# Down phase of a transformer block: one of seven products stays in PSUM, weight sums in place, weight buffers opened earlier

## The chip, the core and the metric

The kernel runs on one core of one Trainium2 chip. The metric is the device time of one execution in microseconds (us), as the median of several. PE is TensorE, DVE VectorE, ACT ScalarE, POOL GpSimd and SP SyncE; SP and POOL issue the large transfers.

## The reference

One layer of an encoder, 512 tokens, width 2048, float32:

```
p = rmsnorm(x) @ W_in                  # six groups of 1024 columns
A = differential attention, 8 heads    # softmax(q1 k1) - lam softmax(q2 k2), then rmsnorm per head
N = neighbourhood attention, 8 heads   # banded softmax with a bias
x = x + concat(A, N) @ W_out           # 2048 x 2048
u = rmsnorm(x) @ W_up                  # 2048 x 8192
x = x + square(relu(u)) @ W_down       # 8192 x 2048
out = rmsnorm(x) * g
```

The change touches the last two matrix products and, through the size of shared tiles, the code ahead of them.

## The kernel before

Every float32 operand is split in two fp32r parts: `hi` is a cast on ACT (L94), `lo` is source minus `hi` on DVE (L95). A product then takes three matmuls: hi·hi, hi·lo, lo·hi. For W_up and W_down the kernel computes a 2x2 block product by Strassen's scheme in Winograd's form, with seven products in place of eight, and sums of weight blocks and of operand blocks as the operands.

The stages, in time: projections and attention; the out-projection (to about 841 us); the **up phase** (841 to 1491.5, 32 column groups `q`, each 7 products of 24 matmuls 128x256, L588); the **down phase** (1491.5 to 2156, L741); the end. The down phase runs over 8 chunks `c` of the hidden width and in each over 2 halves `n` of the output columns. A *half* is seven products of 24 matmuls 128x512; the products are named here by their operand, o[0] to o[6]. Each product needs two weight units of 512 KB, each cut into `wh` and `wl`; 12 matmuls go with a unit. There are three buffers each for `wh` and `wl`.

A scheduler orders the instructions of each engine in advance; within that order an engine waits for semaphores. `tc.high_priority` moves weight loads and splits ahead in it. What a tile pool's free space allows decides how far: the pools of the up phase are closed and those of the down phase opened between the two (L617 to L621), and `wd`, with 11 units of 4 KB per partition, holds all weight loads of the down phase.

In a half, products add into three PSUM tiles of two banks, `pU`, `pV`, `pW`. The scheme needs partial sums: `pU` takes o[0], o[2], o[4], o[6] one after the other, and after each the tile is added into its part of `y` (L753, DVE; `y` is the 512x2048 sum in SBUF). Two of the seven results per half leave by another way: a copy to `st` on ACT (L750) and a DMA of POOL that adds it into `y` (L751). The weight sums are made so: t1 is b11 loaded a second time with b12 added by a POOL DMA (L662 to L663), t2 = t1+b22 and t4 = t2+b21 are DVE sums into fresh tiles (L669).

The order of products in a half:

```
prod(pU, o[0], w11, True)   # then copy and DMA into y
prod(pW, o[1], w1, True)
prod(pU, o[2], w2, False)
prod(pW, o[3], next(ops), False)
prod(pU, o[4], next(ops), False)
prod(pV, o[5], next(ops), True)
prod(pU, o[6], next(ops), False)
```

Operands of attention, out-projection, up and down phase share the pool `tpool`: 4 slots of 16 KB per partition. `mixT` (attention's output, the out-projection's operand) has four such tiles, each of two pairs of heads; `mix_pair` (L432 to L438) loads an earlier pair back from DRAM and splits it. At the start of the up phase, L553 to L565 make its seven operands from `H`.

Of the kernel before, what the change touches and what calls it, by code (L numbers as in the profile page):

```python
# [35 lines left out]
def hymba_kernel(ctx: ExitStack, tc: tile.TileContext, x, x_t, norm_mix_g, w_dq, w_dk, w_dv, w_nq, w_nk, w_nv, lams,  # L36
# [5 lines left out]
    tpool = ctx.enter_context(tc.tile_pool(name="tpool", bufs=4))  # L42
# [72 lines left out]
    hT = [tpool.tile([P, 2, 4, SEQ], F32R, name=f"hT{i}", tag="T") for i in range(4)]  # L115

    def hT_k(kt, hl):
        return hT[kt // 4][:, hl, kt % 4, :]
# [32 lines left out]
    with tc.tile_pool(name="start", bufs=4) as sp, tc.high_priority(offset=20000):  # L151
        acc = sp.tile([P, 2 * SEQ], F32, name="acc", bufs=1)
        xs = []
        for u in range(4):
# [8 lines left out]
            for k in range(4):  # L163
                g, hi = gT[:, 4 * u + k:4 * u + k + 1], hT[u][:, 0, k, :]
                nc.scalar.mul(hi, xt[:, k, :], g)
                nc.vector.scalar_tensor_tensor(out=hT[u][:, 1, k, :], in0=xt[:, k, :], scalar=g, in1=hi.bitcast(F32),  # L166
                                               op0=ALU.mult, op1=ALU.subtract)
# [28 lines left out]
    with es:  # L196
# [128 lines left out]
        def mixed(h, i, o):  # L325
# [102 lines left out]
    hpool = up_es.enter_context(tc.tile_pool(name="hpool", bufs=2))  # L428
    early = up_es.enter_context(tc.tile_pool(name="early", bufs=1))

    def mix_pair(h):
        with tc.high_priority(offset=3000):  # L432
            mf = wpool.tile([P, 2, SEQ], F32, name="mf", tag="raw")
            nc.sync.dma_start(out=mf, in_=mixd[h].rearrange("i p s -> p i s"))
            m, ks = mixT[h // 2], slice(h % 2 * 2, h % 2 * 2 + 2)
            nc.scalar.copy(out=m[:, 0, ks, :], in_=mf)
            eng = nc.gpsimd if h % 2 else nc.vector
            eng.tensor_sub(out=m[:, 1, ks, :], in0=mf, in1=m[:, 0, ks, :].bitcast(F32))  # L438


    H = [hpool.tile([P, 2, 8, 256], F32, name=f"H{i}", tag="H") for i in range(2)]

    def operand(pool, name, tag):

        return pool.tile([P, 2, 8, 256], F32R, name=name, tag=tag)

    def split_s(o, src, neg=False, cuts=1):
        n = 8 // cuts
        for i in range(cuts):
            ks = slice(i * n, i * n + n)  # L450
            if neg:
                nc.scalar.mul(o[:, 0, ks], src[:, ks], -1.0)
                nc.vector.scalar_tensor_tensor(out=o[:, 1, ks], in0=src[:, ks], scalar=-1.0,
                                               in1=o[:, 0, ks].bitcast(F32), op0=ALU.mult, op1=ALU.subtract)
            else:
                split(o[:, 0, ks], o[:, 1, ks], src[:, ks])
# [40 lines left out]
    with tc.tile_pool(name="trans", bufs=2) as tr:  # L497
        for n in range(4):
# [7 lines left out]
            for u in range(8):  # L506
# [3 lines left out]
                for t in range(NT):  # L510
                    ts = slice(t * P, (t + 1) * P)
                    for k in range(2):
                        kt = 2 * u + k
                        m = mixT[kt // 4]
# [371 lines left out]
```

## Time and profile before

| | us |
|---|---|
| median of 3 runs | 2173.17 (2172.59 to 2174.12) |
| profiled execution, its own time | 2174.77 |
| its span, first to last instruction | 2173.0 |
| PE busy | 2094.5 (96%) |
| DVE busy | 1544.0 (71%) |
| ACT busy | 988.1 (45%) |
| mean granted clock of TensorE | 0.984 |

The rows and sums below are those of the profiled execution. Its time is 1.77 us more than its span (start and end of the program) and 1.6 us more than the median. A busy PE is read with care: matmul rows overlap, so that what PE lost in a stretch is the stretch less its matmuls times their spacing.

### The profile page before, as it was taken

How to read it: one execution, taken by the hardware profiler on the slowest of the kernel's cores; microseconds unless marked ns; L12 is line 12 of the kernel's file. 1: busy time of each engine (PE TensorE's matmuls, PEld its weight loads, DVE VectorE, ACT ScalarE, POOL GpSimd, SP SyncE). 2: the span in 40 equal slices, each digit the busy share in tenths (PEclk: the TensorE clock that was granted, in tenths of full speed). 3: DMA queues.
4: the chain of work that ended last, by engine and by line, in shares of the span. 5: the costliest groups of instructions: out<-in, count | busy, mean ns of one | idle time of the engine just before them, and what ended most of it. 6: DMA issues, size and time to landing. Idle time of an engine off the chain costs nothing.

```text
span 2173.0 us, 31223 instructions
## 1 busy us (share of the span) xinstructions
PE 2094.5 (96%) x12604; PEld 1867.4 (86%) x12604; DVE 1544.0 (71%) x1710; ACT 988.1 (45%) x1339; POOL 285.1 (13%) x273
## 2 busy tenths in 40 slices
PE   7999999999999998999999999996999999999995
PEld 6989989989888887999999999995787887787874
DVE  6656556556485437778777877775688798789778
ACT  4444444445354534444444444443455455455444
POOL 4221222122221000000000000000111111111110
PEclk8999999999999999999999999998999999999998
DMA  6332232232233731344334434337798999899983
GB/s 213 121 100 90 96 108 86 94 111 78 92 117 116 271 126 59 120 142 141 123 125 146 136 127 136 131 124 235 199 251 232 232 254 246 234 245 240 246 209 111
DMA packets 114417, 340.30 MB, mean 157 GB/s; under 512 B 11808, under 2 KB 28384, under 8 KB 114272
## 3 DMA queue, kind: packets, MB, share of 16 engines
q1 hardware_dynamic: 87360, 257.07, 35.3%
q0 software_dynamic: 26480, 80.70, 17.1%
q8 instruction: 99, 1.62, 0.3%
q10 hardware_dynamic: 432, 0.53, 0.1%
q14 instruction: 46, 0.38, 0.1%
HBM read 291.06 MB, written 30.25 MB: 148 GB/s over the span
## 4 chain that ended last, share of the span: by engine, by line
PE 84%; DMA 6%; DVE 6%; ACT 2%; issue 1%; SPq 0%; ACTq 0%; DVEq 0%; POOLq 0%
PE pm L588 29%; PE pd L741 19%; PE pa L141 8%; PE pa L99 7%; PE pa L98 7%; PE pa L100 7%; DMA b<-in_w_down 6%; DVE wl L95 2%; PE pb L100 1%; PE pb L98 1%; PE pb L99 1%; PE pc L99 1%; PE pc L100 1%; PE pc L98 1%; DVE y L753 1%
## 5 line engine op out<-in xcount | busy, mean ns | idle before, releaser
L741 PE MATMUL pd<-wh,uT 128*128 128x512 f32 x1792 | 558.2, 393 | 9.3 <-ACT wh L94 8.6
L94 ACT CAST wh<-b 128x1024 fp32r<-128x1024 f32 x256 | 268.6, 1049 | 386.2 <-PE pd L741 215.0
L741 PEld LDWEIGHTS pd<-wh,uT 128*128 128x128 f32 x1792 | 339.8, 190 | 81.3 <-ACT wh L94 9.2
L741 PE MATMUL pd<-wl,uT 128*128 128x512 f32 x896 | 354.2, 395 | 31.0 <-DVE wl L95 30.8
L95 DVE TENSOR_TENSOR wl<-b,wh 128x1024 fp32r<-128x1024 f32 x256 | 311.2, 1219 | 62.9 <-ACT wh L94 60.8
L94 ACT CAST wh<-ts 128x1024 fp32r<-128x1024 f32 x192 | 200.0, 1051 | 291.7 <-PE pm L588 180.7
L95 DVE TENSOR_TENSOR wl<-ts,wh 128x1024 fp32r<-128x1024 f32 x192 | 232.7, 1221 | 131.0 <-ACT wh L94 130.7
L588 PE MATMUL pm<-s,wh 128*128 128x256 f32 x1536 | 281.0, 284 | 3.5 <-ACT p L593 2.2
L588 PE MATMUL pm<-a,wh 128*128 128x256 f32 x1536 | 273.9, 282 | 0.8 <-ACT wh L94 0.8
L588 PEld LDWEIGHTS pm<-s,wh 128*128 128x128 f32 x1536 | 239.5, 191 | 3.9 <-ACT p L593 2.4
L588 PEld LDWEIGHTS pm<-a,wh 128*128 128x128 f32 x1536 | 235.0, 189 | 1.0 <-ACT wh L94 1.0
L741 PEld LDWEIGHTS pd<-wl,uT 128*128 128x128 f32 x896 | 169.8, 190 | 75.4 <-DVE wl L95 40.6
L89 ACT CAST wh<-raw 128x1024 fp32r<-128x1024 f32 (+1 forms) x129 | 134.5, 1043 | 200.2 <-PE pa L99 72.1
L588 PE MATMUL pm<-s,wl 128*128 128x256 f32 x768 | 218.3, 284 | 0.0
L141 PE MATMUL pa<-wh,hT 128*128 128x256 f32 x1024 | 201.1, 291 | 14.7 <-DVE hT L166 8.0
L588 PE MATMUL pm<-a,wl 128*128 128x256 f32 x768 | 211.5, 281 | 0.0
L90 DVE TENSOR_TENSOR wl<-raw,wh 128x1024 fp32r<-128x1024 f32 (+1 forms) x98 | 120.9, 1235 | 117.0 <-ACT wh L89 115.6
L100 PE MATMUL pa<-hT,wl 128*128 128x512 f32 x512 | 201.5, 393 | 0.0
L99 PE MATMUL pa<-hT,wh 128*128 128x512 f32 x512 | 201.2, 393 | 0.0
L98 PE MATMUL pa<-hT,wh 128*128 128x512 f32 x512 | 200.7, 392 | 0.0
L141 PEld LDWEIGHTS pa<-wh,hT 128*128 128x128 f32 x1024 | 167.9, 196 | 19.4 <-DVE hT L166 9.4
L141 PE MATMUL pa<-wl,hT 128*128 128x256 f32 x512 | 147.6, 289 | 0.0
(245 smaller groups left out, 3398.9 us busy)
## 6 DMA issues: line engine op xcount, KB each, us to landing
b<-in_w_down SPq DMA_DIRECT2D x160, 512.0 KB, 5.3
b<-in_w_up SPq DMA_DIRECT2D x128, 512.0 KB, 3.6
b<-in_w_down POOLq DMA_DIRECT2D x64, 512.0 KB, 8.4
raw<-in_w_out SPq DMA_DIRECT2D x32, 512.0 KB, 3.5
ud<-c POOLq DMA_DIRECT2D x32, 512.0 KB, 3.2
ur<-ud SPq DMA_DIRECT2D x32, 512.0 KB, 5.3
y<-st POOLq DMA_DIRECT2D x28, 512.0 KB, 8.1
raw<-in_w_dq SPq DMA_DIRECT2D x16, 512.0 KB, 3.3
```

The costliest lines, as they stand in the source:

```text
L89: nc.scalar.copy(out=wh[:, cs], in_=raw[:, cs])
L90: eng.tensor_sub(out=wl[:, cs], in0=raw[:, cs], in1=wh[:, cs].bitcast(F32))
L94: nc.scalar.copy(out=hi, in_=src)
L95: (eng or nc.vector).tensor_sub(out=lo, in0=src, in1=hi.bitcast(F32))
L98: nc.tensor.matmul(out=ps, lhsT=lh, rhs=rh, start=first, stop=False)
L99: nc.tensor.matmul(out=ps, lhsT=lh, rhs=rl, start=False, stop=False)
L100: nc.tensor.matmul(out=ps, lhsT=ll, rhs=rh, start=False, stop=last)
L141: nc.tensor.matmul(out=ps[t], lhsT=a, rhs=b[:, k, :], start=first and i == 0, stop=last and i == 2, skip_group_check=True)
L588: nc.tensor.matmul(out=ps, lhsT=a[:, k], rhs=b[:, k], start=first and k + i == 0, stop=last and k == 7 and i == 2, skip_group_check=True)
L741: nc.tensor.matmul(out=ps[:, b], lhsT=l, rhs=r[:, k], start=first and u + k + i == 0, stop=last and u == 1 and k == 1 and i == 2, skip_gro ...
L753: nc.vector.tensor_tensor(out=ys, in0=ys, in1=ps, op=ALU.subtract if neg else ALU.add)
```

## The change

The operand pool gets 8 slots of 8 KB in place of 4 of 16 KB; `mixT`, `hT` and the up phase's operands become twice as many tiles. `H[1]` gets a pool of its own, which is closed once the up phase's operands are made; in its place a pool `wd` for weights of the down phase is opened, ahead of the up phase's products. In the down phase, the second product of a half (o[1], with the weights b21) adds up in PSUM over all 8 chunks, in a tile `pv` for each `n`, and is added into `y` once, in the last chunk. `pU` and `pW` are two tiles that swap names from half to half, and the other six products go to them in the order pU, pW, pU, pW, pU, pU. The weight sums are made in place: `ch` holds b11, then by a POOL DMA b11+b12, then by DVE adds + b22 and + b21. b11 is thus loaded once instead of twice. The last half finishes `y` in another order.

```
-    tpool = ctx.enter_context(tc.tile_pool(name="tpool", bufs=4))
+    tpool = ctx.enter_context(tc.tile_pool(name="tpool", bufs=8))
     keep = ctx.enter_context(tc.tile_pool(name="keep", bufs=1))
...
-                    mixT.extend(tpool.tile([P, 2, 4, SEQ], F32R, name=f"mixT{m}", tag="T") for m in range(4))
-                split(mixT[kt // 4][:, 0, kt % 4, :], mixT[kt // 4][:, 1, kt % 4, :], o)
+                    mixT.extend(tpool.tile([P, 2, 2, SEQ], F32R, name=f"mixT{m}", tag="T") for m in range(8))
+                split(mixT[h][:, 0, i, :], mixT[h][:, 1, i, :], o)
...
-    hpool = up_es.enter_context(tc.tile_pool(name="hpool", bufs=2))
-    early = up_es.enter_context(tc.tile_pool(name="early", bufs=1))
+    hpool = up_es.enter_context(tc.tile_pool(name="hpool", bufs=1))
+    early = up_es.enter_context(tc.tile_pool(name="early", bufs=2))
...
-    psD = ctx.enter_context(tc.tile_pool(name="psD", bufs=4, space=bass.MemoryType.PSUM, reuse_waits="tile"))
+    psD = ctx.enter_context(tc.tile_pool(name="psD", bufs=2, space=bass.MemoryType.PSUM, reuse_waits="tile"))
     ypool = ctx.enter_context(tc.tile_pool(name="ypool", bufs=1, reuse_waits="tile"))
-    wd = ctx.enter_context(tc.tile_pool(name="wd", bufs=11, reuse_waits="tile"))
+    wd2 = ctx.enter_context(tc.tile_pool(name="wd2", bufs=3, reuse_waits="tile"))
     y = ypool.tile([P, NT, DM], F32, name="y")
...
-        with tc.high_priority(offset=700):
-            u11, u22, u21, u12 = load(0, 0), load(1, 1), load(0, 1), load(1, 0)
-            pairs = [tpool.tile([P, 2, 2, 4, 256], F32R, name="uT", tag="T") for _ in range(4)]
-            o = [pairs[i // 2][:, i % 2] for i in range(7)]
...
+        with tc.high_priority(offset=700 if c else 250):
+            u11, u12, u21, u22 = load(0, 0), load(1, 0), load(0, 1), load(1, 1)
+            o = [part(u11), part(u12)]
+            nc.vector.tensor_sub(out=u21, in0=u22, in1=u21)
+            o.append(part(u21))
+            f = rx.tile([P, 4, 256], F32, name="uf", tag="b")
+            nc.vector.tensor_add(out=f, in0=u11, in1=u22)
+            o.append(part(f, neg=True))
+            nc.vector.tensor_sub(out=f, in0=f, in1=u12)
+            o += [part(f), part(u11), part(u22)]
...
         def add(a, b):
-            with tc.high_priority(offset=ah):
-                t = wpool.tile([P, 1024], F32, name="ts", tag="raw")
-                nc.vector.tensor_add(out=t, in0=a, in1=b)
-            return t
-
...
-        yield [parts(load(u, 0)) for u in range(2)]
-        t1 = [load(u, 0, 1) for u in range(2)]
-        yield [parts(t) for t in t1]
-        b22 = [load(u, 3) for u in range(2)]
-        t2 = [add(t1[u], b22[u]) for u in range(2)]
-        yield [parts(t) for t in t2]
-        yield [parts(t) for t in b22]
-        t3 = [load(u, 3, 1) for u in range(2)]
-        yield [parts(t) for t in t3]
-        b21 = [load(u, 2) for u in range(2)]
-        t4 = [add(t2[u], b21[u]) for u in range(2)]
-        yield [parts(t) for t in b21]
-        yield [parts(t) for t in t4]
...
+            with tc.high_priority(offset=3000):
+                nc.vector.tensor_add(out=a, in0=a, in1=b)
...
+        ch = [load(wd, "ch", u, 0) for u in range(2)]
+        yield parts(ch)
+        for u in range(2):
+            plus(ch[u], u, 1)
+        b21 = [load(wpool, "raw", u, 2) for u in range(2)]
+        yield parts(b21)
+        yield parts(ch)
+        b22 = [load(wd, "b22", u, 3, bufs=3) for u in range(2)]
+        for u in range(2):
+            add(ch[u], b22[u])
+        yield parts(ch)
+        yield parts(b22)
+        t3 = [load(wd2, "t3", u, 3, 1) for u in range(2)]
+        yield parts(t3)
+        for u in range(2):
+            add(ch[u], b21[u])
+        yield parts(ch)
...
-                    finish(t, 0, None, 0)
-                    times_g(t, 0, 1024)
-            w11, w1, w2 = next(ops), next(ops), next(ops)
-            prod(pU, o[0], w11, True)
-            to_y(pU, 0, 0, False, fresh=True, dma=not end)
-            prod(pW, o[1], w1, True)
+                    finish(t, 0, 1024, 0)
+            prod(pU, o[0], next(ops), True)
+            to_y(pU, 0, 0, False, fresh=True, dma=c < 7)
+            prod(pV, o[1], next(ops), c == 0, c == 7)
+            if c == 7:
+                to_y(pV, 0, 0, False)
+            prod(pW, o[2], next(ops), True)
             to_y(pW, 1, 1, True, fresh=True)
-            prod(pU, o[2], w2, False)
+            prod(pU, o[3], next(ops), False)
             to_y(pU, 0, 1, True, fresh=True)
-            prod(pW, o[3], next(ops), False)
+            if end:
+                for t in (0, 1):
+                    finish(t, 1024, 512, 1)
+            prod(pW, o[4], next(ops), False)
             to_y(pW, 0, 1, True)
+            if end:
+                for t in (0, 1):
+                    finish(t, 1536, 512, 2)
+                    norm_out(t)
+            prod(pU, o[5], next(ops), False)
+            to_y(pU, 1, 1, True)
             if not end:
-                prod(pU, o[4], next(ops), False)
-                to_y(pU, 1, 1, True)
-                prod(pV, o[5], next(ops), True)
-                to_y(pV, 0, 0, False, dma=True)
                 prod(pU, o[6], next(ops), False)
                 to_y(pU, 1, 0, False, fresh=True)
                 continue
...
             for t in (2, 3):
-                finish(t, 1, 1, 2)
-                times_g(t, 1536, 512)
+                finish(t, 1536, 512, 1)
+                scaled(t, 1024, 512)
+                nc.vector.tensor_add(out=ss3[:, t, 0:1], in0=ss3[:, t, 0:1], in1=ss3[:, t, 1:2])
             w4 = next(ops)
...
+                t = 2 + b
                 prod(pU, o[6], w4, False, blocks=(b,))
-                ys = y[:, 2 + b, 1024:1536]
-                nc.vector.tensor_add(out=ys, in0=ys, in1=pU[:, b])
-                finish(2 + b, 1, 0, 1)
-                norm_out(2 + b, 2)
+                ys = y[:, t, 1024:1536]
+                nc.vector.scalar_tensor_tensor(out=ys, in0=pU[:, b], scalar=qs[:, t:t + 1], in1=ys, op0=ALU.mult,
+                                               op1=ALU.add)
+                squares(t, 1024, 512, 1)
+                norm_out(t, late=2, cols=2)
```

The order in which the engines are given their work moves at three places.

**TensorE, between two products of one half** (here the last two of a late half; `pd` is a PSUM tile, `wh`, `wl` weight parts, `uT` an operand). Before, from o[4] to o[5] and from o[5] to o[6]:

```order
L741 MATMUL pd_16367<-wl_16533,uT_16345 128x512
L741 MATMUL pd_16367<-wh_16532,uT_16345 128x512
L741 MATMUL pd_16368<-wh_16569,uT_16345 128x512 [waits Activation_49]
L741 MATMUL pd_16368<-wl_16570,uT_16345 128x512 [waits DVE_49]
...
L741 MATMUL pd_16368<-wh_16573,uT_16345 128x512
L741 MATMUL pd_16367<-wh_16604,uT_16346 128x512 [waits DVE_49,Activation_49]
L741 MATMUL pd_16367<-wl_16605,uT_16346 128x512 [waits DVE_49]
```

After, from o[5] to o[6]; pd_16595 is the next half's first tile:

```order
L768 MATMUL pd_16336<-wl_16531,uT_16330 128x512
L768 MATMUL pd_16336<-wh_16530,uT_16330 128x512
L768 MATMUL pd_16595<-wh_16600,uT_16310 128x512 [waits DVE_49,Activation_49]
L768 MATMUL pd_16336<-wh_16561,uT_16333 128x512 [waits DVE_49]
L768 MATMUL pd_16336<-wl_16562,uT_16333 128x512
```

Before, the product between the two that share pd_16367 has a tile of its own, pd_16368. Now o[5] and o[6] follow each other in pd_16336; the first matmul of o[6] waits for DVE (the sum of o[5] into `y`, L780), and one matmul of the next half stands ahead of it. All 16 halves have this.

**ScalarE, where attention ends** (`pr` are the last differential head's exponentials, `mf` to `mixT0` is the cast of `mix_pair`, `o`, `sq`, `rs` that head's norm). Before:

```order
L294 ACTIVATE pr_5256,l_5258<-pc_5264,nm_5257 128x512
L94 CAST aTh_5208<-pb_5249 128x4x128
L89 CAST wh_6077<-raw_6075 128x1024
L436 CAST mixT0_5051<-mf_6037 128x1024
L436 CAST mixT0_5051<-mf_6071 128x1024
L294 ACTIVATE pr_5279,l_5281<-pc_5282,nm_5280 128x512
L294 ACTIVATE pr_5279,l_5281<-pc_5287,nm_5280 128x512
```

After:

```order
L310 COPY o_5323<-pb_5310 128x512
L312 ACTIVATE sq_5325<-pb_5310 128x512
L94 CAST sqh_5327<-sq_5325 128x512
L320 ACT_TABLE_LOAD
L320 ACTIVATE rs_5334<-pb_5331,eps_sb_83 128x512
L382 ACT_TABLE_LOAD
L382 ACTIVATE lg_5742,nam_5743<-lg_5742,nam_5743 128x256
L94 CAST mixT7_5062<-o_5323 128x512
L436 CAST mixT0_5055<-mf_6048 128x1024
```

The first cast into `mixT0`, which the first matmul of the out-projection waits for, stood ahead of the last exponentials; it now stands behind that head's norm with two table loads.

**SyncE, weight loads of the down phase.** Before, after the last loads of the up phase:

```order
L465 DMA b_14386<-in_w_up 128x1024
L628 DMA ur_14623<-ud_6019 128x4x256
...
L628 DMA ur_15191<-ud_6019 128x4x256
L628 DMA ur_15193<-ud_6019 128x4x256
L661 DMA b_14658<-in_w_down 128x1024
L661 DMA b_14664<-in_w_down 128x1024
```

After, among the first loads of the up phase:

```order
L466 DMA b_7803<-in_w_up 128x1024
L666 DMA b_14691<-in_w_down 128x1024
L666 DMA b_14693<-in_w_down 128x1024
L666 DMA b_14799<-in_w_down 128x1024
L666 DMA b_14801<-in_w_down 128x1024
L666 DMA b_14948<-in_w_down 128x1024
L666 DMA b_14950<-in_w_down 128x1024
L666 DMA b_15056<-in_w_down 128x1024
L466 DMA b_7804<-in_w_up 128x1024
```

Seven loads of W_down (of the first half b11 and b22, of the second b11 and one unit of b22) move to the start of the up phase; b_7804 and b_7805 of W_up stand behind them.

## Rows read from the trace of the kernel before

**Rows 1.** Waits of TensorE in the down phase: total us, times, longest.

```profile
PE pd L741 <- DVE wl L95: 30.8, 21, 16.0
PE pd L741 <- ACT wh L94: 8.6, 2, 4.3
```

**Rows 2.** Stretches: us, then busy (count) of PE, PEld, DVE, ACT, POOL; clock; DMA share, GB/s.

```profile
1491.50:1545.00 53.50, 28.23 (x98) 21.82 (x98) 24.68 (x23) 14.67 (x16) 6.52 (x8) 0.71 0.88 265
1545.00:1570.00 25.00, 25.00 (x112) 20.70 (x111) 16.64 (x14) 12.73 (x13) 3.83 (x4) 1.00 0.80 214
1570.00:2116.00 546.00, 538.46 (x2351) 439.29 (x2349) 454.80 (x393) 277.37 (x274) 79.93 (x81) 1.00 0.91 238
2116.00:2156.00 40.00, 32.49 (x131) 25.71 (x131) 37.59 (x41) 19.01 (x31) 0.00 (x0) 0.91 0.21 60
2156.00:2173.00 17.00, 0.00 (x0) 0.00 (x0) 9.69 (x37) 7.33 (x16) 0.00 (x0) 0.61 0.65 247
```

**Rows 3.** Timeline around the end of the up phase, SyncE's queue, TensorE, VectorE: start, duration.

```profile
1488.30 9.22 SPq L661 DMA_DIRECT2D b<-in_w_down  x11
...
1508.82 0.80 PE L741 MATMUL pd<-wh,uT 128*128 128x512 f32 x1 [4.22 <-ACT wh L94]
...
1520.85 1.23 DVE L638 TENSOR_TENSOR uf<-ur 128x1024 f32<-128x1024 f32 x1 [22.43 <-issue]
...
1525.66 0.79 PE L741 MATMUL pd<-wl,uT 128*128 128x512 f32 x1 [16.05 <-DVE wl L95]
```

**Rows 4.** Timeline at the change from one chunk to the next, VectorE and TensorE.

```profile
1808.50 1.23 DVE L669 TENSOR_TENSOR ts<-b 128x1024 f32<-128x1024 f32 x1 [3.05 <-DMA b<-in_w_down]
...
1812.05 0.50 PE L741 MATMUL pd<-wl,uT 128*128 128x512 f32 x1 [0.56 <-DVE wl L95]
```

**Rows 5.** DMA issues: KB of each, median us from issue to landing.

```profile
b<-in_w_down SPq DMA_DIRECT2D x160, 512.0 KB, 5.3
b<-in_w_down POOLq DMA_DIRECT2D x64, 512.0 KB, 8.4
```

**Rows 6.** Timeline inside the down phase, TensorE and VectorE.

```profile
1550.00 0.62 PE L741 MATMUL pd<-wh,uT 128*128 128x512 f32 x2
...
1550.42 1.22 DVE L753 TENSOR_TENSOR y<-y,pd 128x1024 f32<-128x1024 f32 x1 [0.41 <-PE pd L741]
...
1735.78 1.22 DVE L95 TENSOR_TENSOR wl<-b,wh 128x1024 fp32r<-128x1024 f32 x1
...
1737.05 0.50 PE L741 MATMUL pd<-wl,uT 128*128 128x512 f32 x1 [0.35 <-DVE wl L95]
1737.39 0.63 PE L741 MATMUL pd<-wh,uT 128*128 128x512 f32 x2
...
2133.05 0.50 PE L741 MATMUL pd<-wl,uT 128*128 128x512 f32 x1 [0.99 <-DVE wl L95]
```

**Rows 7.** Timeline from the last attention heads into the out-projection, TensorE, ScalarE, VectorE.

```profile
642.17 1.99 ACT L436 CAST mixT<-mf 128x1024 fp32r<-128x1024 f32 x2
...
648.12 0.39 PE L98 MATMUL pa<-wh,mixT 128*128 128x512 f32 x1
...
662.25 0.39 PE L100 MATMUL pb<-aTh,dv 128*128 128x512 f32 x1
...
670.66 3.34 DVE L321 RECIPROCAL rs<-rs 128x512 f32<-128x512 f32 x1
...
675.06 0.73 DVE L322 SCALAR_TENSOR_TENSOR o<-o,gsub,rs 128x512 f32<-128x512 f32 x1
```

**Rows 8.** Timeline at the start of the up phase, VectorE and TensorE.

```profile
851.63 2.28 DVE L453 SCALAR_TENSOR_TENSOR s<-H,s 128x2048 fp32r<-128x2048 f32 x1
...
853.97 0.58 PE L588 MATMUL pm<-s,wh 128*128 128x256 f32 x1 [1.27 <-DVE s L453]
```

**Rows 9.** Timeline at the end of the program, TensorE and ScalarE.

```profile
2121.71 0.79 PE L741 MATMUL pd<-wl,uT 128*128 128x512 f32 x1 [5.88 <-DVE wl L95]
...
2166.84 1.34 ACT L724 ACTIVATE y<-y,rf 128x512 f32<-128x512 f32 x2 [1.00 <-DVE rf L111]
```

More of the change, by code (lines that the diff above doesn't have):

```diff
@@ L112, in rstd_of @@
         return r
-    hT = [tpool.tile([P, 2, 4, SEQ], F32R, name=f"hT{i}", tag="T") for i in range(4)]
+    hT = [tpool.tile([P, 2, 2, SEQ], F32R, name=f"hT{i}", tag="T") for i in range(8)]
     def hT_k(kt, hl):
-        return hT[kt // 4][:, hl, kt % 4, :]
+        return hT[kt // 2][:, hl, kt % 2, :]
     es = ctx.enter_context(ExitStack())
@@ L586, in prod @@
             for k in range(8):
-                for i, (a, b) in enumerate(((th_, s[:, 0]), (th_, s[:, 1]), (tl_, s[:, 0]))):
-                    nc.tensor.matmul(out=ps, lhsT=a[:, k], rhs=b[:, k], start=first and k + i == 0,
+                for i, (a, j) in enumerate(((th_, 0), (th_, 1), (tl_, 0))):
+                    nc.tensor.matmul(out=ps, lhsT=a[:, k], rhs=s[k // 4][:, j, k % 4], start=first and k + i == 0,
                                      stop=last and k == 7 and i == 2, skip_group_check=True)
@@ L664, in load, with plus @@
             return t
+        def plus(t, u, j):
+            with tc.high_priority(offset=3000):
+                nc.gpsimd.dma_start(out=t, in_=w_down[c, n, u, j], accum_op=ALU.add)
         def add(a, b):
[L667 to L677 removed]
@@ L690, in down_weights, with parts @@
-        yield [parts(t) for t in b21]
-        yield [parts(t) for t in t4]
-    ss3 = keep.tile([P, NT, 3], F32, name="ss3")
+            with tc.high_priority(offset=3000):
+                nc.vector.tensor_add(out=a, in0=a, in1=b)
+        def parts(ts):
+            o = []
+            for t in ts:
+                with tc.high_priority(offset=3000):
+                    h = wpool.tile([P, 1024], F32R, name="wh", tag="wh")
+                    l = wpool.tile([P, 1024], F32R, name="wl", tag="wl")
+                    split(h, l, t)
+                o.append((h.rearrange("p (k c) -> p k c", k=2), l.rearrange("p (k c) -> p k c", k=2)))
+            return o
@@ L708, in times_g, with finish, norm_out @@
         nc.vector.tensor_mul(out=y[:, t, lo:lo + w], in0=y[:, t, lo:lo + w], in1=g)
-    def norm_out(t, late):
-        ss = keep.tile([P, 1], F32, name="ssf", tag="ssf")
-        nc.vector.tensor_reduce(out=ss, in_=ss3[:, t], axis=AX.X, op=ALU.add)
+    def finish(t, lo, w, col):
+        scaled(t, lo, w)
+        squares(t, lo, w, col)
+        times_g(t, lo, w)
+    def norm_out(t, late=None, cols=3):
+        ss = keep.tile([P, 1], F32, name="ssf", tag="ssf", bufs=2)
+        nc.vector.tensor_reduce(out=ss, in_=ss3[:, t, :cols], axis=AX.X, op=ALU.add)
         r = rstd_of(keep, ss, DM, 1, "f")
-        for i in (late, 0, 5 - late, 1):
+        for i in ((0, 1, 2, 3) if late is None else (late, 0, 5 - late, 1)):
             qq = slice(i * 512, (i + 1) * 512)
@@ L731, in hymba_kernel @@
             ops = down_weights(c, n)
-            pU, pV, pW = (psD.tile([P, 2, 512], F32, name="pd", tag="pd") for _ in range(3))
+            pU, pW = (psD.tile([P, 2, 512], F32, name="pd", tag="pd") for _ in range(2))
+            if n:
+                pU, pW = pW, pU
+            if c == 0:
+                pVs[n] = psD.tile([P, 2, 512], F32, name="pv", tag="pv")
+            pV = pVs[n]
             def prod(ps, s, w, first, last=True, blocks=(0, 1)):
@@ L748, in to_y @@
                 elif dma:
[L749 removed]
+                    st = wd2.tile([P, 2, 512], F32, name="st", tag="st", bufs=2)
                     nc.scalar.copy(out=st, in_=ps)
```

114 lines of the change are left out of this document (48 added, 66 removed).

## The prediction

> **What bounds the kernel now.** TensorE is busy 96% of the span, so a change is worth what TensorE stops or starts waiting for. I read the stretches first, then the waits, then the timeline at each wait. A steady stretch gives the scale: two matmuls start 0.45 us apart from the third [rows 6], so one takes 0.225, a product of 24 takes 5.4, a unit 2.7 and a half 37.8. What TensorE lost in a stretch is its length less its matmuls times 0.225. In the 53.5 us after the up phase it ran 98 matmuls, 22.1 us of work: 31.4 lost. In 1570 to 2116 it was idle 546 − 538.5 = 7.5. In 2116 to 2156 it ran 131, 29.5 us of work: 10.5 lost; and 17.0 follow the last matmul [rows 2]. The waits name the cause: 30.8 us for `wl` from DVE in 21 waits, 8.6 for `wh` from ACT in 2 [rows 1]. DVE and the transfers behind it set the edges of the down phase, TensorE its middle.
>
> **Up to down, a gain.** Before, SyncE issues the first eleven weight loads only at 1488.30; TensorE stands 4.2 us at 1508.82 and 16.05 us at 1525.66, behind a DVE that had begun the operand differences at 1520.85 after 22.4 us [rows 3]. Now the first half's b11 and b22 lie in SBUF during the up phase, b21 and the t3 units follow the last W_up loads by SyncE's order, and the operand splits come before the phase ends. What is left by my walk through DVE's order, at 1.2 us per split [rows 6], is one wait: DVE ends the fourth `wl` about 10.1 us into the phase, and TensorE wants it at 8.2. So of 31.4 some 2 stay: **−29** (−31 if none stays, −22 if a landing late by two transfers of 5.3 [rows 5] stays too).
>
> **Chunk by chunk, a gain.** The remaining waits are 19 small ones, most where a chunk begins: at 1808.50 DVE had stood 3.05 us for a weight transfer, and TensorE 0.56 at 1812.05 [rows 4]. A restart costs more than the wait: the matmul after the one at 1737.05 starts 0.34 later, not 0.225 [rows 6]. With 0.11 to 0.15 for each of 19, the 7.5 idle us are some 10 us. The change takes three of sixteen transfers from each half (two second loads of b11, one addition into `y`); the transfer engines were busy 0.91 of this stretch [rows 2]. The in-place sums cost DVE nothing: they are as many as the sums into fresh tiles, 1.23 each [rows 4]. I take **−8.5**, between 0 and −10.
>
> **The end, a gain.** Lost before: 10.5 and 17.0, 27.5 in all [rows 2]. The last half now gives DVE about 43 us of work against TensorE's 37.8: splits of 14 units at 1.14 to 1.2, four sums, six additions into `y`, and the scaling of `y`. Walking both orders I get waits of 1.7 us ahead of o[4], 2.9 ahead of o[6] and 4.3 between the two blocks of o[6], 8.9 together. After the last matmul stand one DVE operation on half a tile (0.75), the squares (0.8), the small operations of the norm (1.5), the last scaling (0.75), the output and the end; the last scaling before ended at 2168.2, 4.8 us ahead of the span's end [rows 9]. With 0.4 to 1.4 for the hand-overs that makes 10. The half before loses 1.4 more, since two scalings of `y` stand ahead of one addition. 8.9 + 10 + 1.4 = 20.3: **−7** (−2 to −12; the 5.88 us wait at 2121.71 [rows 9], which comes from a transfer behind `y`, may keep a part).
>
> **A new wait in every half, a loss.** In TensorE's order o[6] follows o[5] in the same PSUM tile, and its first matmul waits for DVE's addition of o[5]. Before, a product in another tile lay between, 5.4 us that hid the addition. The price: with L the start of a product's last matmul (1550.00), the addition starts at L + 0.42 and takes 1.22; TensorE goes on 0.05 after a DVE end (1735.78 + 1.22 against 1737.05) [rows 6], so at L + 1.69. One matmul of the next half fills in; without the wait the next would start at L + 0.45. Lost 1.24 and the restart's 0.11, 1.35. Times 15 halves (the last is in the end's sum): **+20** (15 to 26; DVE is not late itself, since the `wl` of o[6] was cut earlier). Nothing behind the waiting matmul can pass it on TensorE.
>
> The Trainium skill, "Perfetto Trace Analysis", section "Optimizing Tensor Performance", asks that independent groups of matmuls rotate through PSUM banks, so that the evacuation of one lies beside the next. The trace of before agrees: with the rotation, the large waits of the down phase are for `wl` and `wh`, 39.4 us in 23 [rows 1], and not for the additions. By the rule the sum would keep its +20; without it the term would be 0.
>
> **From attention into the out-projection, a loss.** Before, ACT made the first casts into `mixT0` at 642.17, and TensorE started the out-projection at 648.12, straight behind the last projection, with the last heads' small work in between. Now that cast stands behind the last differential head's norm. From 648.12 TensorE first does the small work that is ahead in its order, some 6.3 us, with the last product of that head's `pb` 5.8 in. Then come, one behind the other: copy, square and cast (1.7), the low part and its sum by TensorE (1.1), the root (0.7), the reciprocal of 3.34 and the product of 0.73 [rows 7], two casts (0.62 and 1.05), and about 0.9 of hand-overs: the first matmul at +15.9. TensorE idles 9.6. Before, the chain from 662.25 to 675.8 took 13.5 [rows 7] with other work between; by that it idles 15. After longer pauses the granted clock was at 1.2 GHz for some time: a matmul took 0.79 at 1525.66 against 0.39 at 648.12, and 0.91 over 2116 to 2156 means 7.2 us at the lower level [rows 2, 3, 7]. I add 2.5 of its 0.7 to 3.6: **+12** (8 to 18).
>
> **The up phase's start, a loss.** The operand in halves puts two DVE operations of 1.2 more ahead of the one of 2.28 that TensorE waited for (1.27 us at 853.97) [rows 8]: **+3.5** (2 to 6). Seven loads of 512 KB stand ahead of the next W_up loads on SyncE; those land near 882.5 and are wanted near 887: 0. Attention's order up to the junction does not move: 0.
>
> **Sum.** −29 − 8.5 − 7 + 20 + 12 + 3.5 = −9. From the profiled 2174.77 that is 2165.8. The median is 1.6 lower: **2164**.
>
> **Rivals.**
> 1. *The additions are hidden.* If TensorE had enough of the next half ready ahead, or the pause were absorbed by DVE's lag, +20 falls away: 2144. Against it: the order puts just one matmul in between.
> 2. *The start of the down phase is only partly filled.* If b21 or the first operands land late, and a third of the gain stays: +19, 2183. For it: the operands need the last `ud` writes, which no earlier load can pass.
> 3. *The in-place sum is late*, slower than before. `ch` can take b12 only when both its parts are cut. The POOL transfers start 3.0 and 0.5 us ahead of the half, land 8.4 later [rows 5], at +5.4 and +7.9, and the parts must be ready at 10.8 and 13.5, after a cast and a split. It decides at a landing time of about 11.5. Beyond it each half loses 1.5 to 3: +24 to +45, about 2188 to 2205. For it: the transfer engines' 0.91 [rows 2]; against it, three transfers fewer.
> 4. *Each new pause drops the clock.* With 2.5 us for each of 15, +38: 2201. Against it: the matmul at 2133.05, after a wait of 0.99 us, took 0.50, as the one at 1737.05 did after 0.35 [rows 6]; for it, that pauses of 4 us and more did lower it [rows 3]. 1.35 us lies between, nearer to the short ones. The Trainium skill, "TensorE: Matmul & The Clock Gate", section "A second HAM failure mode: psum-queue depth-cycling", tells of short idles between groups of matmuls that make the clock swing; this trace shows no such swing for pauses under 1 us.
>
> **How the numbers follow.** Chances: the forecast 0.64 (own range 2154 to 2172), rival 1 0.10, rival 2 0.10, rival 3 0.11, rival 4 0.05. A range of 2142 to 2183 takes in the forecast, most of rival 1 and half of rival 2, about 8 in 10; it leaves out rivals 3 and 4. A difference under 0.2% (4.3 us) can't be told from none. Faster, under 2168.8, is the forecast's lower nine tenths and rival 1, 0.68, less some for errors that add up: 0.64. Within 0.2% lie the forecast's top and a mild rival 2: 0.17. Slower: 0.19.
>
> **What would show it.** Right: one wait of L768 for DVE's `y` of about 1.2 us in each half; no `wl` wait over 3 us after the up phase; a first out-projection matmul some 10 us late behind a cast into `mixT0`; about 10 us from the last matmul to the end. Wrong: waits for `wh` or `wl` inside the halves at o[2] (rival 3), matmuls of 0.79 after the pauses (rival 4), or an unbroken TensorE at o[6] (rival 1).

## The result, and the profile after

| | before | after |
|---|---|---|
| median, us | 2173.17 (5 runs, 2172.59 to 2178.58) | 2160.79 (5 runs, 2159.49 to 2165.09) |
| profiled execution, its time and span | 2174.77, 2173.0 | 2162.22, 2160.4 |

The ratio is 0.9942, with a 95% interval from 0.9927 to 0.9958: 12.4 us faster, where 9 were forecast. The number was near by luck: the experiments below show that a cause that is not in the sum made all of the gain, and that the terms of the sum came to nothing together, to within some 2 us.

First the stages. TensorE's timeline before at the ends of the out-projection, the up phase and the down phase (start, duration):

```profile
839.24 0.39 PE L100 MATMUL pc<-wh,mixT 128*128 128x512 f32 x1
842.37 0.48 PE L588 MATMUL pm<-a,wh 128*128 128x256 f32 x2
...
1491.26 0.28 PE L588 MATMUL pm<-a,wl 128*128 128x256 f32 x1
1495.88 0.79 PE L741 MATMUL pd<-wh,uT 128*128 128x512 f32 x1 [4.35 <-ACT wh L94]
...
2155.59 0.39 PE L741 MATMUL pd<-wh,uT 128*128 128x512 f32 x1
```

The same places after, and the end of the projections:

```profile
647.39 0.39 PE L100 MATMUL pa<-hT,wl 128*128 128x512 f32 x1
...
663.08 0.80 PE L98 MATMUL pa<-wh,mixT 128*128 128x512 f32 x1 [0.18 <-ACT mixT L436]
...
849.86 0.40 PE L100 MATMUL pc<-wh,mixT 128*128 128x512 f32 x1
...
853.00 0.48 PE L593 MATMUL pm<-a,wh 128*128 128x256 f32 x2
...
1495.12 0.28 PE L593 MATMUL pm<-a,wl 128*128 128x256 f32 x1
1495.23 0.39 PE L768 MATMUL pd<-wh,uT 128*128 128x512 f32 x1
...
2149.67 0.39 PE L768 MATMUL pd<-wh,uT 128*128 128x512 f32 x1
```

From these, with the column groups and the halves cut by counting matmuls (a thirty-second and a sixteenth of them each, from the start of its first). The 3.1 us between the out-projection and the up phase, the same in both, are left out:

| stretch | before | after | change | forecast |
|---|---|---|---|---|
| to the last projection | 647.9 | 647.4 | -0.5 | 0 |
| last projection to the end of the out-projection | 191.3 | 202.5 | +11.1 | +12 |
| up phase, first column group | 29.3 | 32.0 | +2.7 | +3.5 |
| up phase, the other 31 | 619.6 | 610.1 | -9.5 | 0 |
| up to down, with the first half | 69.9 | 49.2 | -20.7 | -29 |
| halves 2 to 15 | 546.2 | 557.9 | +11.7 | -8.5 + 20, and 1.4 of the end's |
| last half and what follows it | 65.7 | 58.3 | -7.4 | -8.4 (the -7 without that 1.4) |

The waits of TensorE after (total, times, longest), which answer to [rows 1]:

```profile
PE pd L768 <- ACT wh L94: 25.3, 16, 7.8
...
PE pm L593 <- ACT wh L94: 7.0, 2, 6.5
...
PE pd L768 <- DVE vf L105: 2.3, 1, 2.3
PE pd L768 <- DVE y L822: 2.1, 1, 2.1
PE pd L768 <- DVE wl L95: 1.9, 3, 1.1
```

The 30.8 us for `wl` are 1.9 now; in their place stand 16 waits for `wh`. The stretches after, which answer to [rows 2] (length, then busy and count of PE, PEld, DVE, ACT, POOL; clock, DMA share, GB/s):

```profile
1495.00:1560.00 65.00, 56.06 (x242) 45.77 (x241) 46.76 (x41) 31.45 (x32) 4.91 (x7) 0.95 0.73 192
1560.00:2095.00 535.00, 518.37 (x2260) 422.75 (x2258) 444.40 (x384) 256.36 (x254) 60.01 (x65) 1.00 0.75 194
2095.00:2150.00 55.00, 48.13 (x192) 38.04 (x192) 49.31 (x69) 24.33 (x39) 1.72 (x2) 0.94 0.34 101
```

The transfer engines fell from 0.91 to 0.75, and the clock held 1.00 through all pauses of the middle. One such pause, on TensorE, ACT and DVE:

```profile
1775.77 0.39 PE L768 MATMUL pd<-wh,uT 128*128 128x512 f32 x1
1776.20 1.04 ACT L94 CAST wh<-b 128x1024 fp32r<-128x1024 f32 x1 [1.67 <-PE pd L768]
1776.20 1.22 DVE L780 TENSOR_TENSOR y<-y,pd 128x1024 f32<-128x1024 f32 x1 [0.41 <-PE pd L768]
1777.30 0.73 PE L768 MATMUL pd<-wh,uT 128*128 128x512 f32 x2 [1.13 <-ACT wh L94]
```

The addition stands where it was forecast, 0.43 behind the start of o[5]'s last matmul, but the wait on record is another: the matmul of the next half that was to fill in waits for ACT's cast, which gets its buffer only when o[5] is done with it. The cast and the addition end within 0.2 us of each other. The pause stands in 15 halves, not in all 16: behind the last there is no next half.

The long wait is in the first half. POOL's additions into weight tiles, ACT's casts that wait for them, and TensorE:

```profile
1490.51 0.90 POOL L673 DMA_DIRECT2D b<-in_w_down  x1 [10.38 <-PE pm L593]
1492.20 0.86 POOL L673 DMA_DIRECT2D b<-in_w_down  x1 [0.80 <-DMA b<-in_w_down]
1493.40 1.72 POOL L673 DMA_DIRECT2D b<-in_w_down  x2 [0.34 <-issue]
1496.83 0.85 POOL L673 DMA_DIRECT2D b<-in_w_down  x1 [1.71 <-DVE wl L95]
...
1510.50 1.04 ACT L94 CAST wh<-b 128x1024 fp32r<-128x1024 f32 x1 [7.95 <-DMA b<-in_w_down]
1511.60 0.80 PE L768 MATMUL pd<-wh,uT 128*128 128x512 f32 x1 [7.80 <-ACT wh L94]
```

In POOL's order the first three are for t3 (two of this half, one of the next), the last two the in-place sums of `ch`. These were issued at 1493.9 and 1496.8 and let the casts start at 1510.5 and 1513.5: some 16.6 us each. The matmul at 1511.60 is the first of the third product; it stands in TensorE's order among those of the second, which wait with it. The transfer engines were full in this stretch (a share of 1.04):

```profile
1488.00:1514.00 26.00, 18.20 (x106) 15.94 (x106) 20.01 (x19) 11.89 (x14) 4.89 (x6) 0.88 1.04 286
```

The last product has two waits, and behind each a stretch at the lower clock:

```profile
2138.76 0.47 PE L768 MATMUL pd<-wh,uT 128*128 128x512 f32 x1 [2.30 <-DVE vf L105]
2145.46 0.50 PE L768 MATMUL pd<-wh,uT 128*128 128x512 f32 x1 [2.13 <-DVE y L822]
```

```profile
2139.30:2142.60 3.30, 3.30 (x9) 2.59 (x8) 2.19 (x11) 1.61 (x4) 0.00 (x0) 0.51 0.47 160
2146.30:2149.60 3.30, 3.30 (x9) 2.61 (x8) 1.57 (x8) 1.54 (x3) 0.00 (x0) 0.50 0.45 168
```

And at the start of the up phase, ACT and TensorE:

```profile
862.45 2.00 ACT L453 ACTIVATE s<-H 128x1024 fp32r<-128x1024 f32 x2 [0.21 <-DVE H L561]
864.36 1.03 ACT L94 CAST wh<-ts 128x1024 fp32r<-128x1024 f32 x1
865.44 0.80 PE L593 MATMUL pm<-s__7317,wh 128*128 128x256 f32 x2 [6.50 <-ACT wh L94]
```

### The profile page after: what moved, and what is told of

Read it like the earlier page. It is cut to its first block, busy times and chain, and to the rows that moved or that the text cites. A ratio compares the mean times of both kernels' runs of the same rounds, so it can differ in the third digit from the quotient of the medians.

```text
span 2160.4 us, 31131 instructions
## 1 busy us (share of the span) xinstructions
PE 2087.9 (97%) x12604; PEld 1859.9 (86%) x12604; DVE 1546.9 (72%) x1721; ACT 973.7 (45%) x1328; POOL 265.8 (12%) x257
## 4 chain that ended last, share of the span: by engine, by line
PE 88%; DVE 4%; DMA 3%; ACT 2%; issue 2%; POOL 0%; SPq 0%; ACTq 0%; DVEq 0%; POOLq 0%
PE pm L593 28%; PE pd L768 20%; PE pa L141 8%; PE pa L98 7%; PE pa L99 7%; PE pa L100 7%; PE pv L768 3%; DMA b<-in_w_down 2%; DVE wl L95 1%; PE pb L99 1%; ACT wh L94 1%; PE pb L100 1%; PE pb L98 1%; PE pc L100 1%; PE pc L98 1%
## 5 line engine op out<-in xcount | busy, mean ns | idle before, releaser
L94 ACT CAST wh<-b 128x1024 fp32r<-128x1024 f32 x320 | 335.8, 1050 | 496.0 <-PE pd L768 260.1
L768 PE MATMUL pd<-wh,uT 128*128 128x512 f32 x1536 | 484.8, 393 | 30.5 <-ACT wh L94 25.3
L95 DVE TENSOR_TENSOR wl<-b,wh 128x1024 fp32r<-128x1024 f32 x320 | 389.2, 1221 | 110.7 <-ACT wh L94 108.5
L768 PEld LDWEIGHTS pd<-wh,uT 128*128 128x128 f32 x1536 | 289.9, 189 | 98.4 <-ACT wh L94 32.0
L768 PE MATMUL pd<-wl,uT 128*128 128x512 f32 x768 | 301.1, 392 | 1.9 <-DVE wl L95 1.9
L593 PE MATMUL pm<-a,wh 128*128 128x256 f32 x1536 | 267.2, 279 | 0.5 <-ACT wh L94 0.5
L95 DVE TENSOR_TENSOR wl<-ts,wh 128x1024 fp32r<-128x1024 f32 x128 | 154.9, 1223 | 108.2 <-ACT wh L94 106.8
L94 ACT CAST wh<-ts 128x1024 fp32r<-128x1024 f32 x128 | 132.5, 1051 | 186.5 <-PE pm L593 170.5
L141 PEld LDWEIGHTS pa<-wh,hT 128*128 128x128 f32 x1024 | 168.4, 197 | 18.7 <-DVE hT L166 9.0
L768 PEld LDWEIGHTS pd<-wl,uT 128*128 128x128 f32 x768 | 145.1, 189 | 34.4 <-DVE wl L95 4.7
```

The lines of the kernel that those rows point to most:

```text
L94: nc.scalar.copy(out=hi, in_=src)
L95: (eng or nc.vector).tensor_sub(out=lo, in0=src, in1=hi.bitcast(F32))
L141: nc.tensor.matmul(out=ps[t], lhsT=a, rhs=b[:, k, :], start=first and i == 0, stop=last and i == 2, skip_group_check=True)
L593: nc.tensor.matmul(out=ps, lhsT=a[:, k], rhs=s[k // 4][:, j, k % 4], start=first and k + i == 0, stop=last and k == 7 and i == 2, skip_gro ...
L768: nc.tensor.matmul(out=ps[:, b], lhsT=l, rhs=r[:, k], start=first and u + k + i == 0, stop=last and u == 1 and k == 1 and i == 2, skip_gro ...
```

## The experiments

The kernel before ran beside the experiments: its median was 2171.78 for e1 to e4, 2171.01 for e5 to e8 and 2172.45 for e9 to e11, and the ratios below are to it. The changed kernel's 2160.79 was measured beside 2173.17, so a difference to it can be off by some 2 us.

**The up phase, and 32 bytes.** The up phase's matmuls are the same in both kernels, but for operands that are cut into two tiles, and no wait stands in its last 31 groups in either. The counts of matmuls in 900 to 1480, where TensorE never stops, before and after:

```profile
900.00:1480.00 580.00, 580.00 (x4877) 580.00 (x4876) 441.35 (x438) 244.09 (x321) 15.96 (x30) 1.00 0.40 133
```

```profile
900.00:1480.00 580.00, 580.00 (x4953) 580.00 (x4952) 443.86 (x442) 246.38 (x326) 15.82 (x30) 1.00 0.41 134
```

TensorE's pace itself is 1.6% higher at a clock of 1.00. By operand, three matmuls on the up phase's a11, s1_ and a22 take 0.352 to 0.355 us from start to start before and 0.340 to 0.341 after; on a12, s2, s3, s4 it is 0.36 in both. The addresses of the two programs tell one difference that holds for just those three: they lie above a pool of small norm tiles, which the change made 32 bytes longer (`ssf` got a second buffer; the column that `ss3` got moves nothing). Before they started at multiples of 64 bytes, after at 32 past one, as the weights `wh`, `wl` and the lower operands do in both. (a11 and s1_ also moved down by 16 KB; e1 leaves that out.)

*e1*, the kernel before with that buffer alone:

```
-        ss = keep.tile([P, 1], F32, name="ssf", tag="ssf")
+        ss = keep.tile([P, 1], F32, name="ssf", tag="ssf", bufs=2)
```

> The kernel before with one more 4-byte buffer in the pool of small norms, which moves every buffer above it (the up phase's operands a11, s1_ and a22 among them) by 32 bytes; nothing else moves. In the two traces three matmuls on a11, s1_ and a22 start 0.352 us apart before and 0.341 after, on the four operands below that pool 0.36 in both. Theory: the 32 bytes are the cause, since they put these operands at 32 past a multiple of 64, as the weights lie; then the up phase loses 0.28 us per column group, 9 us in all, and the median falls to about 2164. Rival: the cause is the cutting of the operands into tiles of 8 KB, which this kernel does not have; then the up phase and the time stay, 2173.

Measured: 2162.5 against 2171.78, ratio 0.9951 (0.9933 to 0.997). In the same stretch:

```profile
900.00:1480.00 580.00, 580.00 (x4952) 580.00 (x4952) 449.56 (x448) 249.62 (x328) 15.79 (x30) 1.00 0.41 134
```

One tile of 4 bytes gives the up phase its 9.6 us, and brings the kernel before within 2 us of the changed one.

*e5*, the changed kernel moved back to multiples of 64:

```
     ss3 = keep.tile([P, NT, 4], F32, name="ss3")
+    pad = keep.tile([P, 8], F32, name="pad")
+    nc.vector.memset(pad, 0.0)
```

> The changed kernel with 32 bytes more in the pool of small norms, which puts the buffers above it back on multiples of 64 as in the kernel before. Theory from the shift of the kernel before (2171.8 to 2162.5, up phase 9.6 us shorter): the change owes most of its gain to those 32 bytes; without them the up phase takes 9 us more and the median comes to about 2169, within 3 us of the kernel before. Rival: the gain of the shift belongs to the old layout alone, and this kernel stays at 2161.

Measured: 2171.7 against 2171.01, ratio 1.0001 (0.999 to 1.0011): no difference to the kernel before is left that these runs can tell.

```profile
900.00:1480.00 580.00, 580.00 (x4873) 580.00 (x4872) 437.13 (x435) 242.52 (x319) 15.47 (x29) 1.00 0.40 132
```

*e9*, the changed kernel with weights and operands moved together:

```
+    const.tile([P, 8], F32, name="edge")
     eps_sb = const.tile([P, 1], F32, name="eps_sb")
```

> The changed kernel with 32 bytes more at the start of SBUF, which moves weights and operands together: all lie on multiples of 64 now, none 32 past. Theory: what counts is how the operand lies against the weights; together they stay fast, the up phase stays at 642 us and the median at 2161. Rival: an operand on a multiple of 64 is slow by itself (0.352 to 0.355 for three matmuls in the two kernels that had it); then the up phase takes 652 and the median is 2171.

Measured: 2161.17, ratio 0.9952 (0.9933 to 0.9971); up phase 642.0.

```profile
900.00:1480.00 580.00, 580.00 (x4954) 580.00 (x4953) 443.84 (x442) 247.23 (x325) 16.00 (x30) 1.00 0.40 134
```

So neither place is slow by itself: it counts how operand and weights lie against each other. The fourth pairing, weights on a multiple of 64 and the operand 32 past one, was not run.

*e10*, the control: the kernel before with `bufs=3`, 64 bytes.

> The kernel before with 64 bytes more in the pool of small norms, against the 32 of the first shift: a control. Theory: only the place within 64 bytes counts, so nothing changes: up phase 649, median within 3 us of the kernel before. Rival: any move of these buffers away from their old places helps, by where they lie among each other; then 2163 as with 32 bytes.

Measured: 2169.36 against 2172.45, ratio 0.9992 (0.9979 to 1.0004), up phase 649.4, as before.

```profile
900.00:1480.00 580.00, 580.00 (x4872) 580.00 (x4872) 441.15 (x439) 244.52 (x321) 15.47 (x29) 1.00 0.40 133
```

*e6*, why four operands stay at 0.36: the pool of weights moved to the upper end of SBUF.

```
-    wpool = ctx.enter_context(tc.tile_pool(name="wpool", bufs=3))
+    wpool = ctx.enter_context(tc.tile_pool(name="wpool", bufs=3, side="right"))
```

> The changed kernel with the pool of raw weights, wh and wl at the upper end of SBUF instead of ahead of the operand pool; all tiles still lie 32 past a multiple of 64. Three matmuls on operands in the lower 107 KB took 0.36 us in every trace, on those above 146 KB 0.34 or 0.352. Theory: 0.36 comes from operands and weights that lie in the same part of SBUF; then the four slow operands of the up phase come to 0.34 and the three fast ones may go to 0.36: the up phase changes by -5 to -20 us, and 2161 falls to 2141 to 2156. Rival: the place of the operand alone decides; then the up phase stays within 2 us.

Measured: 2171.73, ratio 1.0000 (0.9989 to 1.0011): some 11 us slower than the changed kernel. By operand, a12 and s2 came down to 0.341, s3 and s4 to 0.349, and a11, s1_ and a22 went up to 0.354 to 0.356; the up phase was 2.1 us shorter, less than the theory's 5 to 20 and just over the rival's 2.

```profile
900.00:1480.00 580.00, 580.00 (x4966) 580.00 (x4965) 445.50 (x445) 247.08 (x325) 15.47 (x29) 1.00 0.41 135
```

The direction is the theory's, operands apart from the weights are faster, but the projections ended 6.0 us later and the first matmul to the last of the down phase took 4.8 us more. What decides the part of SBUF, and why s3 and s4 came only half way, stays open.

**The pause in each half.** *e2* puts o[6] behind the next half's first product:

```
-                prod(pU, o[6], next(ops), False)
-                to_y(pU, 1, 0, False, fresh=True)
+                def last_product(prod=prod, to_y=to_y, pU=pU, s=o[6], ops=ops):
+                    prod(pU, s, next(ops), False)
+                    to_y(pU, 1, 0, False, fresh=True)
+                late.append(last_product)
+                if c == 7:
+                    late.pop()()
...
             to_y(pU, 0, 0, False, fresh=True, dma=c < 7)
+            if late:
+                late.pop()()
```

> The changed kernel with the product of o[6] put behind the next half's first product (not in the last chunk), so that another tile lies between o[5] and o[6]. Theory: the 1.3 us pause in each half comes from this order alone, by DVE's addition and, at the same moment, by ACT's cast for the one matmul of the next half that stands ahead; 14 pauses of about 1.4 go, 2160.8 falls to about 2141. Rival: the pause is ACT's, which gets a free weight buffer only when o[5] ends; then it stays in another place, and the time stays within 5 us of 2161.

Measured: 2148.36, ratio 0.9893 (0.9875 to 0.9911), 12.4 us below the changed kernel. Its waits in the down phase:

```profile
PE pd L769 <- ACT wh L94: 9.7, 2, 8.1
...
PE pd L769 <- DVE wl L95: 4.6, 7, 1.2
```

The pauses are gone (16 waits for `wh` became 2: the first half's, and one in the last chunk, whose order stayed), so they came from the order. Most of halves 2 to 14 alternate between 38.1 and 39.2 us now: once per chunk there is a loss of about 1.2 for `wl`, start to start, that the pauses had covered. In the profiled executions halves 2 to 15 fell by 14.4 us together; this loss is most of the rest of the expected 20.

**The junction.** *e3* hands out mixT7's slot early:

```
                     mixT.extend(tpool.tile([P, 2, 2, SEQ], F32R, name=f"mixT{m}", tag="T") for m in range(8))
+                    nc.gpsimd.memset(mixT[7][:, 0, 0, 0:1].bitcast(F32), 0.0)
```

> The changed kernel with one element per partition of mixT7 written when the mixT tiles are made, so that the operand pool hands out mixT7's slot early and that of mixT0 behind it. Theory: the pool hands its slots out in the order of first writes, and mixT0 had to wait for mixT7, whose first write is the end of the last differential head; then the out-projection starts straight behind the last projection, and 11 us of the 15.7 between them come back: about 2150. Rival: the casts are behind that head because ACT has no time earlier; then 2161 stays.

Measured: 2154.51, ratio 0.992 (0.9905 to 0.9936), 6.3 us below the changed kernel. ACT makes the cast at 640.55 now, and TensorE goes from the last projection to the out-projection without a gap:

```profile
648.13 0.39 PE L100 MATMUL pa<-hT,wl 128*128 128x512 f32 x1
648.36 0.39 PE L98 MATMUL pa<-wh,mixT 128*128 128x512 f32 x1
```

The 11.3 us of this stretch come back, as the theory has it; 2.9 of them are lost again in the up phase, 1.1 of these in its first column group, and 0.85 at its end. The theory's place is right, its total was not.

**The start of the down phase.** *e7* takes the early loads away, by opening the pool in the space that the up phase frees:

```
-    wd = ctx.enter_context(tc.tile_pool(name="wd", bufs=4, side="right", reuse_waits="tile"))
...
+    wd = ctx.enter_context(tc.tile_pool(name="wd", bufs=4, reuse_waits="tile"))
     wd2 = ctx.enter_context(tc.tile_pool(name="wd2", bufs=3, reuse_waits="tile"))
```

> The changed kernel with the pool of weight sums opened behind the up phase, in its freed space, so that no W_down load can start during it. Theory: the early loads are what shortens the first half from 64.8 to 48.8 us; without them it is 60 to 66 again and the run 2172 to 2178. Rival: the earlier operands do it, since DVE began the differences only at 1520.85 before; then the first half stays within 4 us of 48.8.

Measured, one execution: 2172.68, first half 58.8 us. Cut as in the table, the first half takes 65.2 us before and 49.1 after. So the loads are worth 10 of these 16 us; the earlier operands and the rest of the change must be the other 6, which no run takes apart. The 4.35 us for which TensorE stood ahead of the first matmul before are gone without the early loads too: here it starts 0.11 behind the up phase's last.

*e4* takes all four additions of the first half from POOL's queue:

```
+        b12 = [load(wd2, "t3", u, 1) for u in range(2)] if c == n == 0 else None
         for u in range(2):
-            plus(ch[u], u, 1)
+            if b12:
+                add(ch[u], b12[u])
+            else:
+                plus(ch[u], u, 1)
...
-        t3 = [load(wd2, "t3", u, 3, 1) for u in range(2)]
+        t3 = b12 or [load(wd2, "t3", u, 3, 1) for u in range(2)]
+        if b12:
+            for u in range(2):
+                add(t3[u], b22[u])
```

> The changed kernel with the first half's weight sums b11+b12 and b22+b12 made on DVE from a loaded b12, in place of four additions by POOL's transfers. Theory: the 7.80 us wait at the third product of the first half is the in-place sum that lands late (its two transfers took some 16 us behind three other additions on POOL's queue); without it the wait goes, with the clock's fall behind it 9 us in all: about 2152. Rival: DVE is full there (four more operations of 1.2), and the wait moves to wl: 2157 to 2163.

Measured: 2159.91, ratio 0.9947 (0.9931 to 0.9964), no difference to the changed kernel (0.9942) that can be told. The rival has it; the wait is now for DVE, at the next unit:

```profile
1512.63 0.80 PE L775 MATMUL pd<-wl,uT 128*128 128x512 f32 x1 [3.80 <-DVE wl L95]
```

**The repairs together.** *e8* is e2 and e3 in one.

> The changed kernel with both repairs, o[6] behind the next half's first product and mixT7's slot handed out early. If they are independent their gains add: 12.4 and 6.3 from 2160.8 make 2142. Rival: the weights and operands at the start of the down phase become the edge once TensorE comes earlier to it, as the up phase gave back 3 us when the junction was repaired; then 2145 to 2148.

Measured: 2142.76, ratio 0.9864 (0.9842 to 0.9885), 18.0 below the changed kernel where 18.7 were expected: the gains add. *e11* also makes t3 of the first half on DVE, so that the in-place sums have two transfers fewer ahead:

```
-        t3 = [load(wd2, "t3", u, 3, 1) for u in range(2)]
+        first = c == n == 0
+        t3 = [load(wd2, "t3", u, 1 if first else 3, None if first else 1) for u in range(2)]
+        if first:
+            for u in range(2):
+                add(t3[u], b22[u])
```

> Both repairs, and the first half's t3 made on DVE from a loaded b12, so that two additions fewer stand ahead of the in-place sums on POOL's queue. Theory: those sums then land some 5 us earlier, as the additions ahead of them are what made them 16 us long; the first half falls from 48.0 to about 43 and the median from 2142.8 to 2137. Rival: DVE is the next edge in the first half, as when all four sums were put on it; then 2141 to 2144.

Measured: 2139.62, ratio 0.9851 (0.9833 to 0.9869), the lowest median, though its runs (2136.67 to 2142.46) overlap those of e8 (2141.0 to 2143.33), and so do the intervals. The wait at the third product of the first half, in e8, with ACT ahead of it:

```profile
1502.61 1.04 ACT L94 CAST uT<-ur 128x1024 fp32r<-128x1024 f32 x1 [9.44 <-DMA ur<-ud]
1503.56 1.99 ACT L94 CAST wh<-b 128x1024 fp32r<-128x1024 f32 x2
1504.66 0.80 PE L770 MATMUL pd<-wh,uT 128*128 128x512 f32 x1 [5.75 <-ACT wh L94]
```

Here the sums were no longer what came last: they had landed at 1497.8 and 1500.7, and the casts of both stood on ACT behind the cast of an operand, whose transfer landed at 1502.6. In e11 the wait at this place is gone, and others stand ahead of the first matmul and at the products behind:

```profile
1490.11 0.47 PE L774 MATMUL pd<-wh,uT 128*128 128x512 f32 x1 [1.89 <-DVE c L614]
...
1508.02 0.49 PE L774 MATMUL pd<-wh,uT 128*128 128x512 f32 x1 [1.14 <-ACT wh L94]
1511.03 0.79 PE L774 MATMUL pd<-wh,uT 128*128 128x512 f32 x1 [2.51 <-ACT y L780]
```

The sums took 9.2 and 9.5 us to land in e11, 12.0 and 12.3 in e8: fewer additions ahead go with a shorter landing, as the theory has it. The first half fell by 2.5 us, half of what was expected, but TensorE came to it 2.3 us later, counted from the up phase's first matmul: the up phase is 1.1 longer, and from its last matmul to the next it is 2.16 in place of 0.96, behind DVE. So DVE, the rival's engine, took nearly all of it back, and what lies between the two medians is not traced.

## Why the prediction came out near, point by point

- **Up to down, -29.** Right in direction, -20.7 measured. The step that failed is "is one wait: DVE ends the fourth `wl` about 10.1 us into the phase". The wait was ACT's, 7.80 us for the in-place sum of the first half: rival 3's mechanism, in one half of sixteen. I had priced its landing at the median of 8.4 [rows 5] after an issue 3.0 us ahead of the half, and had not counted the three additions ahead on POOL's queue. The first sum was issued 1.3 ahead and took 16.5 to land, beyond the 11.5 from which that rival decides. How much of the 16.5 is POOL's queue and how much the full transfer engines (1.04) no run takes apart; SyncE's transfers of those microseconds landed late as well (a load of W_down issued at 1491.36 took 15.5). My bound of -22 does not come out of its own terms either: 31.4 less 2 less two transfers of 5.3 is 18.8. (Rival 3's upper time is off too: 2164 + 45 is 2209.)
- **Chunk by chunk, -8.5.** Start to start, TensorE lost 12.4 us beyond its pace in 1560 to 2116 before, and little but the pauses after (the `wl` waits are 1.9 us in 3). But e2 shows that a loss of 1.2 per chunk for `wl` comes back when the pauses go: some 7 us of this gain came only because the new wait covered that loss, where the prediction had the two apart. So taking the wait away gave 14.4 us, not its 20.
- **The new wait, +20.** Right in place and price: 1.3 us and the restart's 0.11, against 1.35, in the 14 halves of the middle. Not foreseen was that the matmul which fills in has a wait of its own, for ACT's cast, that ends at almost the same time. Which of them would hold alone was not tried; the order that brings both is the cause by e2. Here the Trainium skill, "Perfetto Trace Analysis", section "Optimizing Tensor Performance", agrees with the runs: two groups in one PSUM tile cost the pause, and a group in another tile between them takes it away.
- **The clock, rival 4.** Ruled out: 1.00 over 1560 to 2095, with all pauses of 1.3 us in it. A stop of 7.8 us did lower the clock (0.80 for the matmul at 1511.60, the level of 1.2 GHz), and the stops of 2.30 and 2.13 in the last product were followed by 0.51 and 0.50. They are shorter than the 4 us from which the prediction had seen the clock fall. The swing of which the Trainium skill, "TensorE: Matmul & The Clock Gate", section "A second HAM failure mode: psum-queue depth-cycling", tells did not show at one such pause per 39 us.
- **Attention into the out-projection, +12.** Right: first matmul 15.7 us behind the last projection (15.9 forecast), +11.1 in all. The cause behind the order, the pool's slots handed out by first write, is from e3, whose edit is only that first write.
- **The up phase's start, +3.5.** Size right, 2.7. The place was one engine over: TensorE waited 6.5 us for a cast of weights (864.36) that stood on ACT behind the operands' splits, which waited for DVE.
- **The end, -7.** The total is right, by luck: -7.4 for the last half with what follows, against -8.4 (half 15 carries the other 1.4, and took 41.0 us against some 39.6 for its neighbours); 10.4 us from the last matmul's end to the span's end against 10. TensorE lost 9.6 us in the last half against 8.9, but the waits cost only 6.2 of that (1.4 at o[3], 2.5 ahead of o[6] and 2.3 between its blocks; forecast were 1.7 at o[4], 2.9 and 4.3). Nearly all of the other 3.4 is in matmuls that start 0.43 apart in place of 0.227, at the lower clock behind the last two waits, which the prediction had at nothing.
- **What was not in the sum.** -9.5 in the up phase, from where 32 bytes put the operands. The sentence that failed is "Attention's order up to the junction does not move: 0" as far as I let it stand for the whole rest: I looked at which instructions move and not at which addresses do. With that term out the change gives 0 by e5 (ratio 1.0001, give or take 2.3 us) and -3.1 by the table's other rows: my sum of -9 for them was 6 to 9 us too good, 8.3 of it at the start of the down phase. That this miss and the missing term are of one size is luck.

## What to carry to other kernels

When a change moves the size of any buffer, compare the pace of a stretch that it should not touch: a count of matmuls in a fixed window finds in one row what no wait shows. Where a gain can't be traced to a wait, undo the byproducts of the change first (here by a pad of 32 bytes) and see whether the gain stays, before the edit is credited. And a new order of products or tiles should be read for the neighbours that it makes: two groups in one PSUM tile, or two tiles whose first writes come in the wrong order from one pool, cost here more than the edit gained, and moving one product and one element gave 18 us back (e8).

## What the runs showed of the hardware that was not expected

Matmuls 128x256 of fp32r ran at a pace that depends on how the moving operand lies to the weights in SBUF. With the same place within 64 bytes, both at 32 past (after, e1) or both at 0 (e9), three took 0.340 to 0.341 us; with 32 bytes between them 0.352 to 0.355 (before, e5, e10). With operand and weights both in the lower 107 KB it was 0.36, whatever else; with the weights moved to the top, 0.341 to 0.349 for those and 0.354 to 0.356 for the others (e6). Additions by POOL's transfers, 8.4 us to land in the median before, took 16.5 with three others issued within 3.5 us ahead of them, 12.0 and 12.3 in e8 and 9.2 and 9.5 in e11, all with the transfer engines full (a share of 1.04 to 1.06). Pauses of 1.3 us every 39 us left the granted clock at 1.00; single stops of 2.13 and 2.30 us were followed by 0.50 and 0.51, the level of 1.2 GHz.
